# How long past the head of an RMSNorm-and-matmul kernel do loads, casts and transposes keep their lead over the stores?

## The chip, the cores and the metric

One core of a Trainium2 chip. The metric is the device time of one execution in microseconds (us); lower is better. Each kernel was timed several times beside runs of the kernel before on the same chip, and a profile was taken of one execution of each. "Span" is the time from the first to the last instruction of a profile.

## The reference

```python
# x: (8, 1024, 768) f32; gamma: (768,); w_qkv: (768, 2304) f32
rms = np.sqrt(np.mean(x ** 2, axis=-1, keepdims=True) + eps)
x_norm = x / rms * gamma
return np.matmul(x_norm, w_qkv).astype(np.float32)
```

The 8192 rows are 64 row tiles of 128. The kernel multiplies the unnormalised tile, in bf16, with weights that already carry gamma, and applies 1/rms when it moves a result out of PSUM.

## The kernel before

Past the head, a row tile goes through these steps: its input is loaded (SyncE's queue), cast to bf16 (VectorE), transposed by a DMA (SyncE's queue), multiplied (TensorE: 30 weight loads and 30 matmuls), moved out of PSUM ("evicted") in turn by VectorE and ScalarE, and stored (SyncE's queue). Every instruction gets a planned time, and the plan, sorted by time, is the order of each engine's program. Engines and SyncE's queue work through their programs in order, so a planned time decides only what stands ahead of what. "Lands" means that a transfer's data have arrived.

The first six tiles and the sixteen pieces of weights form the "head", which has a hand-made plan. After it a loop plans the other 58 tiles:

```python
    def load_x(t):
        X[t] = xin.tile([P, K], f32, name="x_t")
        nc.sync.dma_start(out=X[t], in_=xf[t * P:(t + 1) * P, :])
    # ...
    def xbar(t):
        XT[t] = xTp.tile([P, KO, P], bf16, name="xT")
        nc.sync.dma_start_transpose(out=XT[t], in_=XB[t])
    # ...
    US = 6 * 0.2158 / 512
    now, flip = HEAD_END, 0
    for t in range(HEAD, MT):

        ahead = 6.0 if t < HEAD + 5 else 0.0
        if ("x", t) not in {q[1:] for q in LOADS}:
            at(now - 15 - ahead, load_x, t)
        at(now - 8.5 - ahead, cast, t)
        at(now - 7.5 - ahead, xbar, t)
        at(now - 5, stat, t)
        at(now - 3, recip, t)
        for n0 in range(0, N, NT):
            at(now, mm, t, n0, range(KO))
            now += width(t, n0) * US
            flip ^= 1
            evac_at(now + 0.2, t, n0, "DVE" if flip else "ACT", gap=1.2)
```

`ahead` is the lead. In the head and just after it, SyncE's queue has a backlog (weights, inputs and the first stores: tile 8's transpose took 8.98 us to land, the median of all is 4.3), so the first tiles are asked for 6 us earlier. `HEAD` is 6, and the lead drops to 0 at tile 11. One part of the head matters later: in its list of first loads, the input ("x", 5) and transpose ("t", 5) of tile 5, the last tile of the head.

## Time and profile before

| | kernel before |
|---|---|
| time, three runs | 389.03, 389.21, 389.84 us |
| span of the profile | 387.4 us at a granted clock of 1.000 (the share of TensorE's full clock) |
| TensorE busy | 98% |
| step from one tile to the next | 5.834 us |
| HBM read and written | 32.25 and 75.50 MB |

A busy TensorE bounds the kernel. What the order of loads can change is whether the operand of a tile is there when its turn comes. In the views below, PEld is TensorE's loading of weights, the first to touch a tile's transposed input, and SPq is SyncE's queue.

### The profile page before, as it was taken

Reading aid. Unit: us, or ns where it says so; the run is one execution under the profiler, and the core shown is the slowest. Engines: PE = TensorE matmul, PEld = TensorE weight load, DVE = VectorE, ACT = ScalarE, POOL = GpSimd, SP = SyncE. Lnnn points to the kernel's source line nnn. Section 1 sums busy time; section 2 is a strip of 40 time slices with the busy share of each in tenths; the row PEclk is TensorE's granted clock in tenths of the full one; section 3 lists DMA queues with packets and bytes.
Section 4 is the critical chain, followed back from the end, with each engine's and each line's share of the span. In section 5 each row is a group of like instructions: output and inputs, shape, how many; then the busy total and the mean of one; then the engine's idle time right before and its main releaser. Section 6 shows DMA issues by size and latency. Waiting matters only on the chain.

```text
span 387.4 us, 5456 instructions
## 1 busy us (share of the span) xinstructions
PE 379.7 (98%) x1921; PEld 191.6 (49%) x1959; DVE 153.2 (40%) x307; ACT 181.5 (47%) x365; POOL 6.5 (2%) x14
## 2 busy tenths in 40 slices
PE   7999999999999999999999999999999999999996
PEld 3444654454554554554554554554554554554553
DVE  2744524344333343333343333343333343333332
ACT  4753644444444544444544444534434535434532
POOL 0130000000000000000000000000000000000000
PEclk9999999999999999999999999999999999999999
DMA  7999999999999999999999999999999999999975
GB/s 278 391 274 399 394 321 370 309 383 306 293 315 303 299 314 297 297 310 317 311 294 286 294 336 293 305 319 271 313 320 300 297 326 289 293 332 280 307 257 190
DMA packets 89575, 119.91 MB, mean 310 GB/s; under 512 B 52422, under 2 KB 61388, under 8 KB 89548
## 3 DMA queue, kind: packets, MB, share of 16 engines
q1 hardware_dynamic: 89536, 119.56, 101.0%
q8 instruction: 15, 0.25, 0.3%
q14 instruction: 12, 0.10, 0.1%
q10 hardware_dynamic: 12, 0.00, 0.0%
HBM read 32.25 MB, written 75.50 MB: 278 GB/s over the span
## 4 chain that ended last, share of the span: by engine, by line
PE 89%; DMA 8%; issue 1%; ACT 1%; DVE 1%; SPq 0%; DVEq 0%
PE pm L234 89%; DMA x_t<-in_x_dram 3%; DMA w_f<-in_w_qkv_dram 2%; DMA xT<-xb 2%; DMA out_dram<-ot 1%; ACT ot L253 1%; DVE ot L251 0%; DVE xb L174 0%; SPq L160 0%; SPq L155 0%; SPq L257 0%; DVEq L356 0%; ACT w_b L168 0%
## 5 line engine op out<-in xcount | busy, mean ns | idle before, releaser
L234 PE MATMUL pm<-w_b,xT 128*128 128x512 bf16 (+1 forms) x1882 | 372.3, 357 | 2.1
L234 PEld LDWEIGHTS <-xT 128*128 128x128 bf16 x1920 | 187.6, 98 | 185.8 <-DMA xT<-xb 0.8
L251 DVE TENSOR_SCALAR ot<-pm,rstd 128x512 f32<-128x512 f32 (+1 forms) x161 | 111.5, 694 | 206.2 <-PE pm L234 201.8
L253 ACT ACTIVATE ot<-pm,rstd 128x512 f32<-128x512 f32 (+2 forms) x160 | 102.8, 643 | 192.6 <-PE pm L234 146.5
L185 ACT ACTIVATE sq<-x_t 128x768 bf16<-128x768 f32 x64 | 53.3, 833 | 2.9 <-DMA x_t<-in_x_dram 2.9
L174 DVE CAST xb<-x_t 128x768 bf16<-128x768 f32 x61 | 33.2, 544 | 13.8 <-DMA x_t<-in_x_dram 13.7
L187 ACT ACTIVATE rms<-ssq,eps_sb 128x1 f32<-128x1 f32 x64 | 18.8, 294 | 2.1
L185 ACT ACTIVATION_READ_ACCUMULATOR sq<-x_t 128x1 f32 x64 | 12.2, 191 | 0.0
L166 DVE TENSOR_SCALAR w_b<-w_f,g_sb 128x512 bf16<-128x512 f32 (+1 forms) x16 | 7.7, 498 | 7.1 <-DMA w_f<-in_w_qkv_dram 7.1
L192 DVE RECIPROCAL rstd<-rms 128x1 f32<-128x1 f32 x64 | 9.8, 153 | 0.0
L170 POOL TENSOR_SCALAR w_b<-w_f,g_sb 128x512 bf16<-128x512 f32 (+1 forms) x8 | 5.8, 734 | 24.1 <-DMA w_f<-in_w_qkv_dram 24.1
L286 PE MATMUL pm<-const-bfloat16-1.0 128*128 128x512 bf16 (+1 forms) x14 | 5.3, 533 | 0.8 <-PEq L342 0.8
L168 ACT ACTIVATE w_b<-w_f,g_sb 128x512 bf16<-128x512 f32 (+1 forms) x6 | 3.6, 612 | 2.7 <-DMA w_f<-in_w_qkv_dram 2.7
L212 PE MATMUL pm<-ident_f,x_t 128*128 128x128 f32 x18 | 2.5, 276 | 1.4 <-DMA x_t<-in_x_dram 1.4
L212 PEld LDWEIGHTS pm<-ident_f,x_t 128*128 128x128 f32 x18 | 2.1, 143 | 2.4 <-DMA x_t<-in_x_dram 2.1
L176 ACT CAST xT<-pm 128x256 bf16<-128x256 f32 (+1 forms) x5 | 2.3, 456 | 1.7 <-PE pm L212 1.5
L286 PEld LDWEIGHTS <-const-bfloat16-1.0 128*128 128x128 bf16 x14 | 1.5, 126 | 2.7 <-issue 2.7
L142 ACT ACT_TABLE_LOAD x1 | 1.3, 1283 | 1.4 <-PEq L342 1.4
L174 DVE CAST xT<-pm 128x512 bf16<-128x512 f32 x1 | 0.7, 691 | 0.9 <-PE pm L212 0.9
L269 DVE COPY g_sb<-pm 128x6 f32<-128x6 f32 x1 | 0.2, 165 | 1.7 <-PE pm L268 1.7
L268 PEld LDWEIGHTS pm<-ident_f,g 6*128 6x128 f32 x1 | 0.2, 177 | 0.8 <-issue 0.8
L174 DVE COPY xT<-pm 128x768 bf16<-128x768 bf16 x1 | 0.6, 558 | 0.0
(12 smaller groups left out, 2.5 us busy)
## 6 DMA issues: line engine op xcount, KB each, us to landing
out_dram<-ot SPq DMA_DIRECT2D x124, 512.0 KB, 3.9
x_t<-in_x_dram SPq DMA_DIRECT2D x64, 384.0 KB, 4.2
out_dram<-ot SPq DMA_DIRECT2D x64, 128.0 KB, 3.2
w_f<-in_w_qkv_dram SPq DMA_DIRECT2D x10, 512.0 KB, 7.4
out_dram<-ot SPq DMA_DIRECT2D x8, 256.0 KB, 2.0
w_f<-in_w_qkv_dram SPq DMA_DIRECT2D x4, 256.0 KB, 7.2
xT<-xb SPq DMA_TRANSPOSE x60, 4.3
w_f<-in_w_qkv_dram SPq DMA_DIRECT2D x2, 384.0 KB, 6.1
```

What stands on the lines that cost most here:

```text
L166: nc.vector.tensor_scalar(out=o, in0=i, scalar1=g, scalar2=None, op0=mult)
L168: nc.scalar.activation(out=o, in_=i, func=AF.Copy, scale=g, bias=0.0)
L170: nc.gpsimd.tensor_scalar(out=o, in0=i, scalar1=g, scalar2=1.0, op0=mult, op1=mult)
L174: nc.vector.tensor_copy(out=out, in_=in_)
L185: nc.scalar.activation(out=sq, in_=X[t], func=AF.Square, accum_out=ssq)
L187: nc.scalar.activation(out=rms, in_=ssq, func=AF.Sqrt, scale=inv_k, bias=eps_sb)
L192: nc.vector.reciprocal(out=r, in_=RS[t])
L212: nc.tensor.transpose(out=PT[t, h][:, ko - k0, :], in_=X[t][:, ko * P:(ko + 1) * P], identity=ident_f)
L234: nc.tensor.matmul(out=PM[t, n0][:, :nl], lhsT=XT[t][:, ko, :], rhs=w_b[:, ko, n0:n0 + nl], start=(b == 1), stop=(b == KO))
L251: nc.vector.tensor_scalar(out=o[:, :d], in0=pm[:, :d], scalar1=RS[t], scalar2=None, op0=mult)
L253: nc.scalar.activation(out=o[:, d:], in_=pm[:, d:nl], func=AF.Copy, scale=RS[t], bias=0.0)
L286: nc.tensor.matmul(out=wps[:, :nl], lhsT=ones[:, :P], rhs=ones[:, :nl], start=True, stop=True)
```

## The change

The lead past the head no longer drops from 6 to 0 at tile 11; it shrinks evenly and reaches 0 at tile 19. The intent is that no tile has to make up the whole lead at once while the backlog of the head is still draining.

```diff
-        ahead = 6.0 if t < HEAD + 5 else 0.0
+        ahead = 6.0 * min(1.0, max(0.0, (HEAD + 13 - t) / 9))
```

## The prediction

> **What bounds the kernel now.** I read the page first, then the chain of waits, then the waits of the weight loads (the first instructions to feel a late operand), and last the timelines around the only such wait found. The page's first part and its DMA row:
>
> ```profile
> PE 379.7 (98%) x1921; PEld 191.6 (49%) x1959; DVE 153.2 (40%) x307; ACT 181.5 (47%) x365; POOL 6.5 (2%) x14
> ...
> DMA  7999999999999999999999999999999999999975
> ...
> PE 89%; DMA 8%; issue 1%; ACT 1%; DVE 1%; SPq 0%; DVEq 0%
> ```
>
> TensorE is busy almost throughout, and 89% of the chain that ended last is its matmuls. The DMA digits are high too, so the question is whether data ever come late for TensorE. The chain in the middle of the span:
>
> ```profile
> 85.10 9.46 PE pm L234 x49
> 94.56 0.05 issue
> 94.61 9.46 PE pm L234 x49
> 104.07 0.05 issue
> 104.12 10.10 PE pm L234 x49
> 114.22 0.05 issue
> 114.27 9.46 PE pm L234 x49
> ```
>
> From 85.10 to 114.27 are 29.17 us with 3 x 49 recorded matmuls; a few records can be missing, and 150 matmuls are five row tiles (30 each: four blocks of 512 columns and one of 256, six steps of k). So a tile takes 29.17 / 5 = 5.834 us. Asked for all waits between 45 us (first tile after the head) and 374 us, the view has these lines on data from DMA:
>
> ```profile
> ACT ot L253 <- DMA x_t<-in_x_dram: 15.2, 8, 1.9
> DVE xb L174 <- DMA x_t<-in_x_dram: 8.5, 4, 3.4
> PEld L234 <- DMA xT<-xb: 0.3, 1, 0.3
> ```
>
> VectorE and ScalarE do wait, but the feed of TensorE waits once, for 0.3 us, in 329 us. The timeline of the weight loads shows where:
>
> ```profile
> 65.92 8.31 PEld L234 LDWEIGHTS <-xT 128*128 128x128 bf16 x44
> 74.50 15.45 PEld L234 LDWEIGHTS <-xT 128*128 128x128 bf16 x79 [0.27 <-DMA xT<-xb]
> ```
>
> At 74.50 tile 11 begins: the first tile whose load, cast and transpose have no lead in the kernel before. SyncE's own timeline there, one row per group of issues (start, length, what):
>
> ```profile
> 58.38 1.58 SPq L221 DMA_TRANSPOSE xT<-xb  x1
> 60.05 1.95 SPq L257 DMA_DIRECT2D out_dram<-ot  x3
> 62.10 1.15 SPq L155 DMA_DIRECT2D x_t<-in_x_dram  x1
> 63.35 2.05 SPq L257 DMA_DIRECT2D out_dram<-ot  x3
> 65.49 1.29 SPq L155 DMA_DIRECT2D x_t<-in_x_dram  x1
> 66.89 0.66 SPq L257 DMA_DIRECT2D out_dram<-ot  x1
> 67.66 2.07 SPq L221 DMA_TRANSPOSE xT<-xb  x1
> ```
>
> Tile 11's input is issued at 62.10 and its transpose at 67.66. Transposes between 60 and 130 us took 4.2/4.5/6.8 us (least, median, most) from issue to landing; the 6.8 is this one, so it landed at 74.46, 0.04 us before the weight load took it. Later tiles are comfortable: tile 20's was issued at 119.30, landed at 123.66 and was used at 126.92, 3.26 us to spare.
>
> **What the Trainium skill says.** Three places bear on this.
> - "TensorE: Matmul & The Clock Gate", section "Wait — 56ns, not 53.3ns?": warm matmuls start N ÷ 2.4 GHz plus about 2.5 ns apart. For a tile that is 24 x 215.8 + 6 x 109.2 ns = 5.83 us (an estimate from that page); the trace has 5.834 us and a granted clock of 1.000. TensorE has no room between its matmuls, so nothing that moves loads can make a tile shorter.
> - "Perfetto Trace Analysis", section "DMA Instruction — HWDGE (DVE, Sync)": the profiled window of such an instruction ends when the sequencer is free, before the data have moved. So I take landings and not the issue rows. The trace agrees: 2.07 us of issue at 67.66, 6.8 us to landing.
> - "DMA: Bandwidth & Descriptors", section "Queues, rings and completion order": each DMA engine consumes its descriptors in ring order. What is issued earlier on SyncE's queue is therefore served earlier, and the cost falls on what is put behind it, here the stores. The landings I read follow the order of issue; no run yet shows what a reorder does.
>
> **The change part by part.** Before, the lead is 6.0 us for tiles 6 to 10 and 0 from tile 11. After, it is 6.0 x min(1, (19 - t) / 9): unchanged for tiles 6 to 10, then 5.33, 4.67, 4.00, 3.33, 2.67, 2.00, 1.33 and 0.67 us for tiles 11 to 18, and 0 from tile 19 on. Only eight of 64 tiles get another place.
>
> No instruction is added or removed. Comparing the two builds' order: TensorE, ScalarE and GpSimd run the same sequence. On VectorE the casts of tiles 11 to 18 come 1 to 4 places earlier; tile 11's passes three evictions. On SyncE the loads of tiles 11 to 17 come 4, 3, 2, 2, 2, 2 and 1 places earlier, the transposes of tiles 11 to 18 come 3, 3, 3, 2, 1, 1, 1 and 1 places earlier, and tile 10's transpose goes one place later, behind the load of tile 11.
>
> Cost: casts (61 x 0.54 us) and DMA bytes are the same; the sum of added work is 0. Gain, for tile 11: its load can follow the store that SyncE finished at about 57.4 us, so it issues near 57.5 instead of 62.10; at the 4.46 us that it took before, it lands at 62.0. Then come tile 10's transpose (58.4 to 60.0), three stores (to 62.0), the load of tile 12 (to 63.2), one store (to 63.7) and tile 11's transpose near 63.8 instead of 67.66. With 4.4 to 6.8 us to landing it is there at 68.2 to 70.6, needed at 74.2: 3.6 to 6.0 us to spare in place of 0.04. That ends the 0.27 us wait.
>
> What of the 0.27 us lies on the path: tile 10 begins at 68.40 and tile 12 at 80.24, 11.84 us for two tiles against 2 x 5.834 = 11.67. So 0.17 us of it reached TensorE's pace; the rest hid in the weight loads' run ahead of the matmuls. The sum: 0 added, 0.17 us removed. From 389.21 that is 389.04 us; I put 389.0.
>
> **The rivals.**
> 1. The blocked cast. VectorE takes its work in order, so a cast moved ahead of evictions stalls them until its input lands; PSUM could fill and stop TensorE. For: the 3.4 us wait in the line above is such a stall. Against: the stalls of tiles 9 and 10 (3.38 us before 50.87, 3.17 us before 57.80) already happen with a lead of 6, and no wait of TensorE follows; the weight loads' only wait is at 74.50. Eight PSUM buffers hold 8 x 1.295 us = 10.4 us of matmul blocks. I expect up to four new VectorE waits of 1 to 3 us, hidden. If not hidden: +0.5 to +2 us, near 390 to 391.
> 2. Delayed stores. The moved loads and transposes push the stores behind them. For: between 45 and 75 us DMA moves 336 GB/s, against 304 GB/s between 132 and 162, so there is a backlog of the head's stores. Against: an output tile has seven buffers of each size, 7 x 5.83 = 41 us, and a load of 384 KB delays a store by about 1.2 us (an estimate at 336 GB/s). Lost time: 0.
> 3. The tight spot only moves, to tile 10 (its transpose goes behind a load) or to tiles 12 to 14. Against: tile 10 had 6.4 us to spare (landed 62.00, used 68.40), the load costs it about 1; tile 12 had 1.31 us and gains three places. Lost time: 0 to 0.2 us, so the time would stay at 389.2.
> 4. A larger gain: with 0.04 us to spare, tile 11 may wait longer in some runs, and the spread of the runs before (389.03 to 389.84) may come from that. Then the median falls by up to 0.5 us, to 388.7. The backlog that varies from run to run lies in the head, however, and the change leaves the head as it is.
>
> **Range and chances.** The one wait on the path is 0.17 us, a twentieth of a per cent; three runs of one kernel spread over 0.8 us. The range runs from 388.6 (rival 4) to 389.6 us (rival 3 or a small part of rival 1, plus the spread). Two per cent is 7.8 us: there is no such time to win while a tile takes 5.834 us for 64 tiles (373.4 of 387.4 us), and to lose it TensorE would need stalls of about a microsecond in each of the moved tiles. Chances: faster 0.5%, within 2% 98.5%, slower 1%.
>
> **What would show it.** Right: in the waits between 45 and 374 us the weight loads' line on the transposes is gone; tile 11's transpose is issued near 64 and lands near 69; tiles start 5.83 us apart from tile 10 on; from about 115 us the trace is the same, with some 3.2 us to spare; VectorE shows a few more waits on inputs up to 75 us; the span is 387.2 us. Wrong: a wait of the weight loads or matmuls on an eviction (rival 1), an eviction that waits for a store (rival 2), or a weight load of another tile that waits for its transpose (rival 3). A time over 390 us would mean that rival 1 took hold.

## The result, and the profile after

| | before | after |
|---|---|---|
| first comparison, six runs each: median | 389.12 us | 388.22 us |
| lowest to highest | 387.91 to 389.88 us | 388.08 to 388.79 us |
| ratio, 95% interval | | 0.9979 [0.9961, 0.9998] |
| profiled run, span | 389.13, 387.4 us | 388.79, 386.8 us |

Ratios are the mean time of one kernel's runs over that of the other's of the same rounds, so they are not quite the ratio of the medians quoted. The profiled run of the changed kernel is one of its six; that of the kernel before (389.13 us) is a further execution, not one of the six. By this comparison the gain is 0.9 us (0.2%), five times what was predicted, though the interval nearly touches 1.

The page of the changed kernel, first parts, to be compared with the prediction's first fence:

```profile
span 386.8 us, 5458 instructions
...
PE 379.2 (98%) x1921; PEld 191.5 (50%) x1959; DVE 153.1 (40%) x307; ACT 181.4 (47%) x365; POOL 6.5 (2%) x14
...
DMA  8999999999999999999999999999999999999975
```

Nothing has moved on this scale. The waits between 45 and 374 us, on data from DMA:

```profile
DVE xb L174 <- DMA x_t<-in_x_dram: 12.6, 5, 3.4
ACT ot L253 <- DMA x_t<-in_x_dram: 7.6, 4, 1.9
```

The weight loads' wait for a transpose is gone from this view. VectorE waits for inputs 12.6 us in five waits instead of 8.5 in four, which is the price named in the prediction, and it stays hidden. SyncE's timeline in the same stretch as before:

```profile
57.03 1.35 SPq L155 DMA_DIRECT2D x_t<-in_x_dram  x1
58.47 1.51 SPq L221 DMA_TRANSPOSE xT<-xb  x1
60.07 1.72 SPq L257 DMA_DIRECT2D out_dram<-ot  x3
61.88 1.21 SPq L155 DMA_DIRECT2D x_t<-in_x_dram  x1
63.20 0.86 SPq L257 DMA_DIRECT2D out_dram<-ot  x1
64.16 1.95 SPq L221 DMA_TRANSPOSE xT<-xb  x1
```

Tile 11's input is issued at 57.03 us instead of 62.10, and its transpose at 64.16 instead of 67.66. By the trace the transpose lands at 70.84 us and is first used at 73.84: 3.00 us to spare instead of 0.04.

Where does the time go, then? The weight loads from 20 to 120 us, before and after (start, length, count, and in brackets the idle time ahead of the row):

```profile
29.57 44.66 PEld L234 LDWEIGHTS <-xT 128*128 128x128 bf16 x240 [0.55 <-DMA xT<-xb]
74.50 45.49 PEld L234 LDWEIGHTS <-xT 128*128 128x128 bf16 x233 [0.27 <-DMA xT<-xb]
```

```profile
29.18 90.90 PEld L234 LDWEIGHTS <-xT 128*128 128x128 bf16 x476 [0.55 <-DMA xT<-xb]
```

The row at 74.50 is gone, and the row at 29 us already starts 0.39 us earlier. That row is tile 5's, long before anything that the change moves. Going further back, the weight loads between 7 and 9 us, before and after:

```profile
7.96 0.64 PEld L212 LDWEIGHTS pm<-ident_f,x_t 128*128 128x128 f32 x6 [1.68 <-DMA x_t<-in_x_dram]
8.57 0.21 PEld L234 LDWEIGHTS <-xT 128*128 128x128 bf16 x2
```

```profile
7.55 0.64 PEld L212 LDWEIGHTS pm<-ident_f,x_t 128*128 128x128 f32 x6 [1.49 <-DMA x_t<-in_x_dram]
8.16 0.21 PEld L234 LDWEIGHTS <-xT 128*128 128x128 bf16 x2
```

The second tile's input came 0.41 us later in the one run, with the same instructions ahead of it. It is a difference of the execution, not of the kernel.

A time can now be split in four: the start of tile 6 (its first weight load), the stretch from there to the start of tile 63, 9.51 to 9.53 us to the end of the span in every trace used below (9.59 in `before_dve16`), and what the device time has beyond the span.

| profile | time | tile 5's transpose lands | tile 6 starts | tile 6 to 63 | outside the span |
|---|---|---|---|---|---|
| before | 389.13 | 29.53 | 45.06 | 332.76 | 1.78 |
| after | 388.79 | 29.14 | 44.67 | 332.59 | 2.01 |
| difference | -0.34 | -0.39 | -0.39 | -0.17 | +0.23 |

So of the 0.34 us between the profiled runs, -0.39 is the head, which the two kernels share; -0.17 is tile 11, as predicted; -0.01 is the end; and +0.23 lies outside the traced span, which nobody expected. The experiments ask three things: whether tile 11 makes the spread of the kernel before (theory A), whether the head does (theory B), and whether tiles 12 to 18 matter at all (theory C).

### The profile page after: what moved, and what is told of

The parts are those of the page before. It is cut to its first block, busy times and chain, and to the rows that moved or that the text cites. A ratio compares the mean times of both kernels' runs of the same rounds, so it can differ in the third digit from the quotient of the medians. Undisturbed runs are those within 1.5% of the kernel's fastest.

```text
span 386.8 us, 5458 instructions
## 1 busy us (share of the span) xinstructions
PE 379.2 (98%) x1921; PEld 191.5 (50%) x1959; DVE 153.1 (40%) x307; ACT 181.4 (47%) x365; POOL 6.5 (2%) x14
## 4 chain that ended last, share of the span: by engine, by line
PE 89%; DMA 8%; issue 1%; ACT 1%; DVE 1%; SPq 0%
PE pm L234 89%; DMA x_t<-in_x_dram 3%; DMA w_f<-in_w_qkv_dram 2%; DMA xT<-xb 2%; DMA out_dram<-ot 1%; ACT ot L253 1%; DVE ot L251 0%; DVE xb L174 0%; SPq L160 0%; SPq L155 0%; SPq L257 0%; ACT w_b L168 0%
```

## The experiments

### The same two kernels again

No edit: the kernel before against itself, and the changed kernel once more.

> The kernel before, unchanged, against itself. Theory A (the wait of tile 11 for its transpose differs from run to run and makes the spread): ratio 1.000, runs spread over 1 us or more between 387.9 and 389.9; the profile of this run shows a wait of the weight loads at tile 11 of a size between 0 and 1.8 us, and a time that goes with it. Theory B (the spread comes from the head or from the chip, whatever the kernel): the same spread, but the wait at tile 11 stays near 0.3 us in every profile and the start of tile 6 moves instead.

> The changed kernel again. Theory A: its runs stay within some 0.3 us of 388.2, and the mean is 0.7 to 1.0 us below the kernel before. Theory B: it spreads over 1 us or more like the kernel before, and the difference shrinks to the 0.17 us that the two traces show.

Measured on one chip: `before_again` 388.12 us median, 387.67 to 390.00, ratio 1.0006 [0.9988, 1.0024]; `after_again` 388.44 us, 388.16 to 388.72, ratio 1.0005 [0.9993, 1.0017]; the kernel before in these rounds 388.39 us (11 runs). The 0.9 us are gone. The changed kernel is where it was (388.22, now 388.44); it is the kernel before that moved, from 389.12 to 388.39. The trace of `before_again`, weight loads:

```profile
20.04 8.30 PEld L234 LDWEIGHTS <-xT 128*128 128x128 bf16 x39
28.84 91.23 PEld L234 LDWEIGHTS <-xT 128*128 128x128 bf16 x479 [0.51 <-DMA xT<-xb]
```

There is no wait at tile 11: the transpose landed 0.74 us before its use, and the stretch from tile 6 to 63 is 332.59 us, that of the changed kernel. Theory B expected a wait of some 0.3 us there in every profile and missed that it can be nothing at all; theory A allowed 0 to 1.8 us. Neither had `after_again` right: its runs spread over 0.56 us where B expected 1 us or more, and it shows none of the 0.7 to 1.0 us that A expected.

### One part of the lead alone

```diff
-        ahead = 6.0 if t < HEAD + 5 else 0.0
+        ahead = 6.0 if t < HEAD + 5 else 16.0 / 3 if t == HEAD + 5 else 0.0          # t11_only
+        ahead = 6.0 if t < HEAD + 5 else 0.0 if t == HEAD + 5 else 6.0 * min(1.0, max(0.0, (HEAD + 13 - t) / 9))   # t12_on
```

> The lead of tile 11 alone (5.33 us, as in the changed kernel); tiles 12 and on have none, as in the kernel before. Theory A: the whole gain, 388.2 us and little spread. Theory C (tiles 12 to 18 lose time too in runs that were not profiled): a part of the gain, 388.4 to 388.9 us. Theory B: no difference beyond 0.2 us.

> The other part: tiles 12 to 18 have the lead of the changed kernel, tile 11 has none. Theory A: no gain, 389.1 us and a spread of 1 us or more; the load of tile 12 now goes out directly behind that of tile 11 and ahead of tile 11's transpose, so it may be a little slower, up to 390. Theory C: a part of the gain. Theory B: no difference beyond 0.2 us.

Measured: `t11_only` 388.20 us, ratio 1.0006 [0.9991, 1.0022]; `t12_on` 387.85 us, ratio 0.9994 [0.9981, 1.0007]. Neither is told apart from the kernel before, and the one without tile 11's lead has the lower time of the two, against theory A. The stretch is 332.59 and 332.60 us, so tiles 12 to 18 lose nothing either (theory C). The profile of `t11_only` happened to fall on its slowest run, 389.96 us:

```profile
24.50 4.54 PEld L234 LDWEIGHTS <-xT 128*128 128x128 bf16 x22 [0.21 <-DMA xT<-xb]
30.55 89.39 PEld L234 LDWEIGHTS <-xT 128*128 128x128 bf16 x469 [1.50 <-DMA xT<-xb]
```

Here is a run as slow as the slowest of the kernel before, and tile 11 has 6.25 us to spare in it. Its excess is in the head: the transpose of tile 5 lands at 30.50 us, the weight loads wait 1.50 us for it (TensorE itself 1.0), and tile 6 starts at 46.04. The other half came earlier: its first weight load of a matmul with weights is at 8.58 us, against 7.72 in `before_third` below, where tile 6 starts at 44.10. A slow run does not need tile 11.

### The wait made large, and the lead kept for good

```diff
-        ahead = 6.0 if t < HEAD + 5 else 0.0
+        ahead = 6.0 if t < HEAD + 5 else -3.0 if t == HEAD + 5 else 0.0     # late11
+        ahead = 6.0                                                         # const6
```

> The kernel before with the load, cast and transpose of tile 11 put 3 us later in the plan (lead -3 in place of 0), all other tiles as before. It makes the wait of tile 11 large on purpose. If a wait there is never made up later (TensorE is the bound, theories A and B alike), the profile shows a wait of the weight loads at tile 11 of 1 to 3 us, the stretch from tile 6 to tile 63 grows from 332.6 us by just that, and the time rises by as much: 389.5 to 391. A rival D, that the slack elsewhere swallows such a wait, expects the stretch to stay at 332.6.

> The lead of 6 us for every tile, so that none loses it. Theory B (the lead past the head is worth the 0.0 to 0.2 us of tile 11 and nothing else): stretch from tile 6 to tile 63 332.6 us, 5 us or more to spare for every tile after the head, and the time equal to the kernel before within 0.3 us. Theory C (later tiles lose time): faster than the changed kernel. If stores put behind loads cost anything, slower.

`late11`: 389.21 us, ratio 1.0029 [1.0010, 1.0049], weight loads:

```profile
28.67 44.66 PEld L234 LDWEIGHTS <-xT 128*128 128x128 bf16 x240 [0.56 <-DMA xT<-xb]
74.29 45.71 PEld L234 LDWEIGHTS <-xT 128*128 128x128 bf16 x234 [0.96 <-DMA xT<-xb]
```

The wait is 0.96 us, just under the 1 to 3 expected, and the stretch is 333.45 us, 0.86 more than 332.59. So about 0.1 us of such a wait is swallowed, as in the kernel before (0.27 seen, 0.17 on the path), and the rest is never made up: rival D falls. The ratio agrees, 0.29% or 1.1 us, within its wide interval.

`const6`: 388.23 us, ratio 0.9998 [0.9980, 1.0016], stretch 332.59 us. Tiles 11 to 21 that have a landing in the trace have 5.99 to 10.88 us to spare, and it buys nothing that is seen. Nor is a cost seen of the stores that stand behind more loads.

### Tile 5 sooner in the head

If the head sets the time, moving tile 5's transpose should move it. Only the list of the first loads is edited:

```diff
-    (-8.85, "w", 10), (-8.84, "x", 5), ... (15.55, "w", 13), (22.65, "t", 5),
+    (-8.85, "x", 5), (-8.84, "w", 10), ... (22.655, "w", 13), (22.65, "t", 5),                       # tile5_sooner
+    (-8.865, "x", 5), (-8.85, "w", 10), ... (22.655, "w", 12), (22.656, "w", 13), (22.65, "t", 5),   # tile5_soonest
```

> The kernel before, with only the head's loads reordered: the input of tile 5 goes out ahead of the eleventh piece of weights, and its transpose ahead of the fourteenth. In all six traces so far the start of tile 6 is the landing of tile 5's transpose plus 15.5 us, and this landing differs by 2 us between runs. Theory B' (that landing sets the time of the whole kernel): it lands about 1.3 us sooner, the wait of the weight loads near 29 us shrinks, tile 6 starts at 43.3 to 44 us, and the time falls by 0.3 to 1 us, to 387.5 to 388.1, with less spread. Theory A (tile 11 makes the spread): no change of the spread.

> The same further: the input of tile 5 ahead of the tenth piece of weights, its transpose ahead of the thirteenth. Theory B': it lands 2.5 us or more sooner and the wait near 29 us is gone; the time falls by 0.3 to 1.3 us, unless the later weights now make a wait of their own, which the profile would show as a wait of conversions and of matmuls on them.

`tile5_sooner`: 388.40 us, ratio 0.9997 [0.9983, 1.0011]. Its trace has one unbroken row of weight loads:

```profile
19.96 100.00 PEld L234 LDWEIGHTS <-xT 128*128 128x128 bf16 x520
```

The transpose of tile 5 lands at 27.28 us and is no longer waited for; tile 6 starts at 43.86, which is 36.49 us after the first weight load of a matmul with weights (7.37). In `before` and `late11`, too, it starts 36.50 and 36.51 us after that one (8.57 and 7.66), although their weight loads waited 0.55 and 0.56 us for tile 5: they run ahead of the matmuls, and TensorE itself waited there less than 0.1 us. The least in any trace is 36.20 us. So the head has two limits close together: 36.2 to 36.5 us of TensorE's own work from its first matmul, and 15.5 us from the landing of tile 5's transpose. Removing the second leaves the first, which begins with the landing of the first inputs, and the timed runs show no gain: they lie between 387.82 and 388.85 us, the kernel before beside them between 387.85 and 389.69. Theory B' was right about the wait and wrong about its worth. At tile 11 a small wait is back: the step from tile 10 to 11 is 0.13 us longer, though the stretch grows by 0.05 us at most, to 332.64.

`tile5_soonest`: 389.66 us, ratio 1.0028 [1.0006, 1.0049], slower, by the turn it was warned of. Waits between 18 and 46 us:

```profile
PEld L234 <- issue: 1.0, 1, 1.0
PE pm L234 <- POOL w_b L170: 0.7, 1, 0.7
```

TensorE now waits for a converted piece of weights, because tile 5's input has pushed the weights back: it lands at 18.85 us in place of 21.61 in `before_third`, and GpSimd begins its part of the tenth piece at 20.31 in place of 19.33. This trace is of a run of 388.50 us; what made the slowest, 391.03 us, was not traced.

### More profiles of both kernels, and the two edits together

> A third profile of the kernel before, to see how large its wait at tile 11 can be. Theory B: 0 to 0.3 us beyond the usual step of 5.83 us between tiles 10 and 11, whatever the time of this run; the time is the start of tile 6 plus 343.9 us (344.1 at most) plus that wait. Theory A: a wait near 1 us in a run that takes over 389 us.

> A fourth profile of the kernel before, with the same expectations: theory B a wait of 0 to 0.3 us at tile 11 and a time that follows the start of tile 6; theory A a wait near 1 us when the run is slow.

> The changed kernel timed again on one more chip. Theory B: between 0 and 0.2 us faster than the kernel before, ratio 0.9995 to 1.0000 within its interval of some 0.0015, no wait at tile 11, stretch from tile 6 to tile 63 332.60 us. Theory A: 0.5 to 1 us faster, ratio near 0.998.

> The changed kernel together with the earlier input and transpose of tile 5 (the milder of the two reorders of the head). The reorder alone ended the wait near 29 us but then showed 0.13 us at tile 11; with the lead past the head that wait should be gone. Theory B': stretch from tile 6 to tile 63 332.60 us, no wait near 29 us, the start of tile 6 at the first matmul plus 36.5 us; time 387.6 to 388.2 us, at most 0.5 us below the changed kernel.

`before_third` and `before_fourth` took 388.02 and 387.99 us, as theory B expected (start of tile 6 plus 343.9 us). `after_third`, on a second chip: 388.16 us, 388.01 to 390.38, ratio 1.0005 [0.9984, 1.0027]; the kernel before beside it 388.31 us (12 runs). `ramp_and_tile5` (the change plus the edit of `tile5_sooner`): 388.03 us, 387.83 to 388.31, ratio 0.9990 [0.9977, 1.0002]. Its trace waits for no transpose from 20 us on, and tile 6 starts 36.26 us after the first such weight load (36.5 expected), but the interval contains 1, so it is not shown to beat either kernel. All profiles of the two kernels in one table:

| profile | time | tile 5's transpose lands | tile 6 starts | tile 6 to 63 | to spare at tile 11 | outside the span |
|---|---|---|---|---|---|---|
| before | 389.13 | 29.53 | 45.06 | 332.76 | 0.04 | 1.78 |
| before_again | 388.23 | 28.80 | 44.34 | 332.59 | 0.74 | 1.78 |
| before_third | 388.02 | 28.44 | 44.10 | 332.60 | 0.06 | 1.80 |
| before_fourth | 387.99 | 28.56 | 44.10 | 332.59 | 0.04 | 1.78 |
| after | 388.79 | 29.14 | 44.67 | 332.59 | 3.00 | 2.01 |
| after_again | 388.72 | 29.02 | 44.55 | 332.60 | 3.08 | 2.05 |
| after_third | 388.11 | 28.38 | 43.98 | 332.59 | 2.40 | 2.01 |

Tile 11 cost the kernel before 0.17 us in one profile of four and nothing in three. The profile that the prediction started from was the worst of the four in its head as well: against the mean of the last two (388.00 us, tile 6 at 44.10) it has 0.96 us in the head and 0.17 at tile 11, together the 1.13 us by which it is slower. Of the 0.96 us, 0.94 are a later first matmul (8.57 us against 7.72 and 7.53). And the 0.04 us in the table is not slack: in `late11`, `before_dve16` and the two reorders of tile 5, too, weight loads that wait for tile 11 begin 0.04 us after the landing. So `before_third` and `before_fourth` were at the edge, and only `before_again` had time to spare.

### What lies outside the span

The last column is 0.2 us higher for the changed kernel in all three profiles, and 1.96 us in `ramp_and_tile5`. The record gives the span of every timed run to 0.1 us (but for the first set of the kernel before), and there it is the same: time less span is 1.88 to 2.06 us in all 23 timed runs with the full ramp (those of the changed kernel and of `ramp_and_tile5`), and 1.73 to 1.86 us in all 64 of the other kernels. The changed kernel has other waiting instructions: its trace counts 438 instructions of all kinds on VectorE and 490 on ScalarE, where the kernel before has 433 and 493. The edits (condensed here) add idle one-column instructions in the middle of the span:

```diff
+    def extra():
+        for _ in range(5):                       # before_dve5; 16 in before_dve16
+            nc.vector.memset(spare, 0.0)
+        # after_act3 and after_act16: 3 or 16 x nc.scalar.activation(out=spare_a, in_=eps_sb, func=AF.Copy)
 ...
+        if t == 40:
+            at(now - 4.5, extra)
```

> The kernel before plus five one-column fills on VectorE in the middle of the span, which nothing reads: 438 instructions on VectorE as in the changed kernel, in place of 433. The time of a run less its traced span was 1.78 to 1.81 us in ten traces of kernels with 432 to 436 VectorE and 492 or 493 ScalarE instructions, and 1.96 to 2.05 us in the four with 438 and 490. Theory E (the count on VectorE makes it): 1.96 us or more here. Theory F (something else in the program makes it): 1.78 to 1.81 us.

> The same with sixteen fills, 449 instructions on VectorE. Theory E with a threshold: about 2.0 us outside the span; theory E with a cost for each instruction: 2.3 us or more; theory F: 1.78 to 1.81 us.

> The changed kernel plus three one-column activations on ScalarE that nothing reads: 493 ScalarE instructions as in the kernel before, VectorE stays at 438. If the fewer ScalarE instructions made the time outside the span longer, it falls to 1.78 to 1.81 us; theory E expects it to stay at 1.96 to 2.05 us.

> The same with sixteen activations, 506 on ScalarE: theory E 1.96 to 2.05 us outside the span; if the count on ScalarE matters, any other value.

Outside the span are 1.78 and 1.74 us in the two built on the kernel before (437 and 448 instructions on VectorE, each one short of what was intended) and 2.04 and 2.04 us in the two built on the changed kernel (493 and 506 on ScalarE). Neither count makes it: theory E falls, and what remains is F, something else that goes with the order of the change. All six traces with the full ramp have 1.96 to 2.05 us, the twelve others 1.74 to 1.81. What it is stays open.

`before_dve16` took 391.22 us, and again the head tells. Its first stretches, then those of the kernel before (columns: window, its length, busy time of PE, PEld, DVE, ACT and POOL, then granted clock, DMA share, GB/s):

```profile
0.00:10.00 10.00, 7.56 (x26) 3.60 (x27) 2.28 (x8) 3.94 (x8) 0.70 (x6) 0.91 0.81 289
10.00:20.00 10.00, 10.00 (x54) 5.38 (x53) 7.01 (x18) 7.43 (x17) 1.69 (x2) 0.92 0.94 340
```

```profile
0.00:10.00 10.00, 7.79 (x34) 3.91 (x35) 2.50 (x8) 4.36 (x10) 0.70 (x6) 1.00 0.81 282
10.00:20.00 10.00, 9.95 (x53) 4.68 (x53) 7.26 (x18) 7.82 (x18) 1.67 (x2) 1.00 1.05 389
```

TensorE was granted 0.91 and 0.92 of its clock in the first 20 us of this execution. Tile 6 starts at 46.89 us, 2.79 later than in `before_third`. It is one run, so it only shows that the head has a further source of spread; the sixteen fills, planned near tile 40, are not blamed for it. The same trace has this at tile 11, whose lead it lacks like the kernel before:

```profile
76.56 43.33 PEld L236 LDWEIGHTS <-xT 128*128 128x128 bf16 x223 [0.51 <-DMA xT<-xb]
```

Its stretch from tile 6 to 63 is 333.00 us, 0.40 over the undisturbed 332.60, while `before_dve5`, with tile 6 at 44.37, has 332.59. So in six traces with the order of the kernel before, tile 11 cost 0.40 us in the one with the latest head, 0.17 in the next latest and nothing in four. Theory A holds in that much: in these two a slow head and a wait at tile 11 come together, with the wait the smaller part.

## Why the prediction was wrong

- **What bounds the kernel: right.** Tiles follow each other at the same pace in both kernels, and 6 us of lead for every tile (`const6`) leave the stretch at 332.59 us.
- **The cost at tile 11: right for that trace.** Predicted 0.17 us, measured 0.17 (332.76 to 332.59). The transpose was predicted to issue near 63.8 us, landing at 68.2 to 70.6; it issued at 64.16 and landed at 70.84, with 3.00 us to spare where 3.6 to 6.0 were expected. The 0.04 us before, read as time to spare, was none. And one trace stood for the kernel: the other three of it lose nothing there. Over the six traces with its order (the two with idle fills included) the mean is 0.57 / 6 = 0.1 us.
- **"The sum: 0 added, 0.17 us removed": incomplete.** The changed program carries 0.2 us outside the traced span, in all its timed runs. "No instruction is added or removed" held for the working instructions, not for waiting ones; the idle fills show that their count does not make the 0.2 us. It is larger than what the change saves, and it fits ratios of 1.0005 that are not below 1; their intervals of at least 0.0012 either way are too wide to show it by themselves.
- **"From 389.21" and the range: the step that failed.** It took three runs of one kernel for its level and their spread of 0.8 us for the whole spread, and set the lower end at 388.6 us. The kernel before has medians of 388.39 and 388.31 us in two later sets, and 387.67 to 390.00 in its own runs of one set. The changed kernel at 388.22 us, and 388.44 and 388.16 in later sets, lay below the range because the level was 0.8 us too high, not because the change gains 0.9. Why that first set was slow is not known: four of its six runs took 389.03 us or more, against three of the 29 timed runs of the kernel before in later sets, so it was hardly an ordinary draw.
- **Rival 4: the right size for the wrong reason.** It allowed a median 0.5 us lower if tile 11 waited longer in some runs. The most that a trace with that order lost there is 0.40 us, beside 2.79 us in its head, and kernels whose traces lack that wait have runs of 389.89 (`const6`), 389.96 (`t11_only`) and 390.38 us (`after_third`), of which only that of `t11_only` is traced. Its own objection, that the varying backlog lies in the head and stays there, was the answer.
- **Rivals 1 to 3: rightly dismissed.** VectorE's stalls grew by 4.1 us and stayed hidden; between 45 and 374 us nothing waited for a store, and no other tile for its transpose.

What stays open: none of the six runs of the kernel before in the first comparison was profiled (the profile is of a seventh), so that the slow ones were slow in the head, and how much of it was tile 11, is argued from other traces, not shown. Whether the chip, the time or chance made that set slow was not tested. And the cause of the 0.2 us outside the span is unknown.

## What to carry to other kernels

Before believing a gain of a few tenths of a per cent, run the kernel before against itself and split each trace at a mark that the change cannot reach: here the stretch from tile 6 to tile 63 repeats within 0.01 us in undisturbed runs, while the head ahead of it differs by 1 us and more. A wait seen once in one trace is worth its length times how often it happens, so look at several traces before pricing it. A prediction of so small a change should centre on several sets of runs of the kernel before, not on one.

## What the Trainium skill lacked or had wrong

- "DMA: Bandwidth & Descriptors", section "DMA Transpose (X-bar)": it has no landing time of a transpose in a queue that is also full of stores. Here it took 4.2, 4.5 and 6.8 us (least, median, most, 60 to 130 us) in the kernel before, and the 6.8 us, while the head's backlog drained, is that of tile 11.
- No page says how much the whole start of a kernel, with its loads, differs between executions; "TensorE: Matmul & The Clock Gate" treats only the moment at which the array's clock rises. The start of tile 6 ran from 43.77 to 46.89 us in profiles of kernels with the same head order, and the latest of these had a granted clock of 0.91 in its first 10 us.
- No page names a part of the device time outside the traced instructions that depends on the order of the program (the nearest, "Runtime: NRT & Kernel Launch", is about other pairs of times): 1.74 to 1.81 us in twelve traces, 1.96 to 2.05 us in the six with the full ramp.
